# Input scaling and score-pad clearing leave GpSimd; the softmax division of the neighbourhood attention moves to ScalarE

## The chip, the cores and the metric

The kernel runs on one core of one Trainium2 chip. Its time is the device time of one execution in microseconds (us); the median of three runs counts. A core has five engines with a queue each, worked off in order: TensorE (PE in the profile; its weight loads are PEld), VectorE (DVE), ScalarE (ACT), GpSimd (POOL) and SyncE (SP), which here issues every data transfer (DMA).

## The reference

One encoder layer over 2048 tokens of width 1024, all in fp32:

```python
h = rmsnorm(x, g_mix)
z = h @ w_in                      # 1024 -> 5648, split into the branches' inputs and the gates
h_m   = mLSTM, forward and backward, from qk_m, v_m, o_m, i_pre, f_pre
h_na  = neighbourhood_attention(q_na, k_na, v_na, rpb)   # 8 heads of 32, window 8 x 16 on a 32 x 64 grid
h_mem = cross attention of q_mem into 256 memory tokens
y = g0 * (h_m @ w_proj_mlstm) + g1 * (h_na @ w_proj_na) + g2 * (h_mem @ w_proj_mem)
x = x + y @ w_out
out = x + square(relu(rmsnorm(x, g_ffn) @ w_up)) @ w_down
```

The change touches two places of it: `rmsnorm(x, g_mix)`, that is x times a factor per channel (`g_mix`) times a factor per token, and the softmax of the neighbourhood attention, `exp(s - max) / sum`.

## The kernel before

Every fp32 product is made of three matmuls (`mm3`, lines 241 to 243): each operand is split into a high part, which ScalarE writes, and a remainder, which VectorE writes. Weights arrive in units of 512 KB (`fetch`): DMA, ScalarE copy (L185), VectorE subtraction (L186). The work has three phases. Phase 1 (`phase_1`, 0 to some 850 us) takes the tokens in four blocks of 512 (`block_a`): it normalises a block, computes the inputs of all branches, and, woven in between, runs the attention into memory (`mem_unit`) and the neighbourhood attention (`na_stream`). Phase 2 is the mLSTM and the gates that are left, phase 3 the merge, the output projection and the MLP.

The order of TensorE's instructions is written out by hand: the program's order is the chip's. After every few matmuls a `tick` lets the woven streams put in one more step. The other engines' queues are ordered at compile time by a planner, which goes by each instruction's place in the program (its priority, which can be shifted, as by `LATER` around the weight splits) and by when it expects the operands to be there. Each queue then runs strictly in that order. In phase 1 the large products (24 matmuls each, `tok_group` and `ch_group`) go to two PSUM banks in turn (`mm=2`), which ScalarE mostly empties.

*Inputs.* Block 0 loads token-major tiles (`load_norm`). For blocks 1 to 3, `prep_x` loads a tile of 128 tokens that lies channel-major, `xT` (128 channels of one of 8 groups on the partitions; per partition 8 groups x 128 tokens), into one of two buffers `xt`, and GpSimd multiplies it twice (L428): by `gmix`, one factor per partition and group, and by `rb`, one factor per token, held in the tile `gbc`. There are 12 such tiles. For blocks 1 and 2 (`GATES_3`) the result is also stored (`s_raw`). `split_part` (L447 on ScalarE, L448 on VectorE) then splits it into `hT`, the operand of the block's matmuls. The factor per token comes from `rms_x`, which loads the same tokens again in the other layout and squares them on ScalarE (L457).

*Scores.* `na_scores` handles one head for 128 queries against 440 keys (320 in the first and last group of rows, g = 0 and g = 7): a matmul into PSUM (L1112), VectorE adds the bias and takes the extreme value in one instruction (L1115) into the score buffer `nsb`, ScalarE takes the exponential and its sum (L1117), VectorE the reciprocal (L1119) and the product with it (L1120, the softmax division), and GpSimd clears the pad behind the scores, up to the next multiple of 120 columns (L1123). There are 128 such heads. `nsb` is a rotating tile of three buffers. Four to five attention steps later `na_transpose` has TensorE transpose the buffer in pieces of 120 columns, pad included (L1131), and ScalarE or VectorE copies it out (L1134, L1136); `na_values` multiplies by the values (L1148). The bias tiles `nab` are loaded by DMA (L1103) into four buffers.

GpSimd's other work in phase 1 is `rstd` (L335, L336) and two products (L970, L1233), which stay.

Of the kernel before, what the change touches and what calls it, by code (L numbers as in the profile page):

```python
# [13 lines left out]
F32 = mybir.dt.float32  # L14
F32R = mybir.dt.float32r
BF16 = mybir.dt.bfloat16
AF = mybir.ActivationFunctionType
ALU = mybir.AluOpType
# [66 lines left out]
class Body:  # L85
# [296 lines left out]
    def phase_1(self):  # L382
        nc, a = self.nc, self.a
        p_a = self.p_a

        nc.scalar.activation(p_a.tile([128, 16], F32, name="warm"), self.mhalf, AF.Exp)
        self.xorder = [(0, t) for t in ORDER_0] + [(b, t) for b in range(1, NB) for t in range(4)]
        self.xhs = []
        self.hT = self.p_h.tile([128, 2, 8, TB], F32R, name="hT", tag="hT", bufs=1)
        self.mem_lanes = [(0,), (2,)]  # L390
        self.streams = [self.unit_stream(self.qkq, [(1, 3)]), self.unit_stream(self.memq, self.mem_lanes), self.na_stream()]
        self.mem_setup()
        self.bif = p_a.tile([16, 1], F32, name="bif")
        nc.sync.dma_start(self.bif, a["b_if"])
        cw = p_a.tile([128, 4, 6], F32, name="cw")
        nc.sync.dma_start(cw, a["conv_wb"])
        self.cw = p_a.tile([128, 4, 6], F32, name="cws")

        nc.vector.tensor_scalar(self.cw[:, 0:2], cw[:, 0:2], 1.0 / 16, None, ALU.mult)
        nc.vector.tensor_scalar(self.cw[:, 2:4], cw[:, 2:4], 0.5, None, ALU.mult)  # L400
        self.gmix = p_a.tile([128, 8], F32, name="gmix")
        nc.sync.dma_start(self.gmix, a["gT_mix"])
        self.halo = p_a.tile([128, 4, 4], F32, name="halo")
        nc.vector.memset(self.halo, 0.0)
        gna = p_a.tile([128, 2], F32, name="gna_raw")
        nc.sync.dma_start(gna, a["g_na"])
        self.gna = p_a.tile([128, 2], F32, name="gna")
        nc.vector.tensor_scalar(self.gna[:, 0:1], gna[:, 0:1], 32 ** -0.5, None, ALU.mult)
        nc.vector.tensor_copy(self.gna[:, 1:2], gna[:, 1:2])
        for b in range(NB):  # L410
            self.na_rate = NA_RATE[b]
            self.block_a(b)
        self.aux_end = self.na_end = True
        self.drain()

    def prep_x(self, gsrc=None, xt=None):

        if self.xorder:
            nc = self.nc
            b, t = self.xorder.pop(0)  # L420
            r0 = b * TB + t * 128
            if b == 0:
                self.xhs.append((self.load_norm(self.a["x"][r0:r0 + 128], self.gbc, gsrc, xt), t, False))
                return
            xt = self.x_tile(self.a["xT"][4 * b + t]).rearrange("p (k t) -> p k t", k=8)
            rb = self.rb[:, t * 128:(t + 1) * 128]
            for y in (self.gmix.unsqueeze(2), rb.unsqueeze(1)):
                nc.gpsimd.tensor_tensor(xt, xt, y.to_broadcast([128, 8, 128]), ALU.mult)  # L428
            if b in GATES_3:
                self.store(self.scr["raw"][b][:, :, t * 128:(t + 1) * 128], xt)  # L430
            self.xhs.append((xt, t, True))
# [674 lines left out]
    def na_scores(self, u, h):  # L1106
        nc = self.nc
        q, k = u["qk"]
        nk, c0 = u["nk"], 24 * u["half"]
        psc = self.ps("mx")  # L1110
        kl = k[:, h, :nk // 40 * 64].rearrange("p (r c) -> p r c", c=64)[:, :, c0:c0 + 40]
        nc.tensor.matmul(psc[:, :nk], q[:, h, u["half"] * 128:u["half"] * 128 + 128], kl, start=True, stop=True)  # L1112
        sb = self.t("nsb", [128, 480], 3)
        mx = self.small(1, "n")
        nc.vector.tensor_tensor_reduce(sb[:, :nk], psc[:, :nk], u["bias"][h][:, :nk], -1.0, 3e38, ALU.add, ALU.min, mx)  # L1115
        sm = self.small(1, "n")
        nc.scalar.activation(sb[:, :nk], sb[:, :nk], AF.Exp, scale=-1.0, bias=mx, accum_out=sm)  # L1117
        rs = self.small(1, "n")
        nc.vector.reciprocal(rs, sm)  # L1119
        nc.vector.tensor_scalar(sb[:, :nk], sb[:, :nk], rs, None, ALU.mult)  # L1120
        kp = len(u["kts"]) * 120
        if kp > nk:
            nc.gpsimd.memset(sb[:, nk:kp], 0.0)  # L1123
        return u, h, sb

    def na_transpose(self, u, h, sb):
# [650 lines left out]
```

## Time and profile before

| | |
|---|---|
| median of 3 runs | 2962.95 us (2962.1 to 2963.0) |
| the profiled execution | 2953.93 us; its span, first to last instruction, 2952.2 us |
| PE busy | 2861.8 us (97%) |
| DVE busy | 2092.6 us (71%) |
| ACT busy | 1218.8 us (41%) |
| POOL busy | 268.4 us (9%) |
| mean granted TensorE clock | 0.990 |

Busy times are shares of the profiled span, summed over phases with different limits. "Idle before, releaser" in a row is the time in which the row's engine did nothing before the instruction, and what ended it. The granted clock (PEclk) is the share of full speed at which TensorE was let run in a stretch. In the timeline several instructions of one line can be merged into one row (x2). DVE instructions that follow each other overlap a little at their ends, so a row can begin before the row above has ended.

### The profile page before, as it was taken

To read this page: it belongs to the slowest core of one execution; us is meant where nothing else is said; L and a number is where in the kernel's file an instruction comes from. 1 tells how busy PE (TensorE), PEld (TensorE's weight loads), DVE (VectorE), ACT (ScalarE), POOL (GpSimd) and SP (SyncE) were. 2 spreads that over 40 slices of the span, in tenths; PEclk is the share of its full clock that TensorE was granted. 3 is DMA by queue.
4 is the path that set the end of the run, shared out by engine and by line. 5 is a ranking of instruction groups with operands and counts; after the bars stand their busy time and mean duration, and the time that the engine had idled before them with its cause. 6 is when DMAs were issued, how large, how long until landed. Compare 5 with 4: busy or idle time off the path is not lost.

```text
span 2952.2 us, 41677 instructions
## 1 busy us (share of the span) xinstructions
PE 2861.8 (97%) x14908; PEld 2353.6 (80%) x14908; DVE 2092.6 (71%) x3490; ACT 1218.8 (41%) x2326; POOL 268.4 (9%) x406
## 2 busy tenths in 40 slices
PE   8999999999899989999999999999999999999999
PEld 7777787777677777888888888888888888888887
DVE  5867768676655667756688888666685988886666
ACT  6555556455433445343243333533312433344331
POOL 4231230320012321000000000000000000000000
PEclk9999999999999999999999999999999999999999
DMA  7866877677887895847435445756863444466554
GB/s 261 273 212 201 251 231 242 216 229 226 268 264 253 275 322 193 313 172 256 140 117 172 153 154 184 258 197 216 293 215 118 148 157 153 149 232 217 194 187 163
DMA packets 341487, 625.42 MB, mean 212 GB/s; under 512 B 29120, under 2 KB 150912, under 8 KB 340768
## 3 DMA queue, kind: packets, MB, share of 16 engines
q1 hardware_dynamic: 341280, 622.76, 64.5%
q8 instruction: 118, 1.93, 0.3%
q14 instruction: 89, 0.73, 0.1%
HBM read 446.03 MB, written 176.62 MB: 211 GB/s over the span
## 4 chain that ended last, share of the span: by engine, by line
PE 82%; DVE 6%; DMA 6%; issue 2%; ACT 2%; SPq 1%; POOL 1%; DVEq 0%; ACTq 0%; POOLq 0%
PE mm L241 25%; PE mm L242 25%; PE mm L243 25%; PE tr L1131 1%; DVE ws L186 1%; DMA nab<-in_rpb_dram 1%; PE pn L901 1%; DMA wr<-in_w_units_dram 1%; ACT ws L185 1%; PE mx L1148 1%; PE mx L1112 1%; PE pn L904 1%; DVE nsb L1115 1%; PE mm L1540 0%; DMA og<-s_o 0%
## 5 line engine op out<-in xcount | busy, mean ns | idle before, releaser
L242 PE MATMUL mm<-X,ws 128*128 128x512 f32 x1032 | 401.6, 389 | 1.4 <-DVE X L1368 1.4
L241 PE MATMUL mm<-X,ws 128*128 128x512 f32 x1032 | 401.9, 389 | 0.0
L243 PE MATMUL mm<-X,ws 128*128 128x512 f32 x1032 | 401.5, 389 | 0.0
L211 ACT ACTIVATE ws<-wr 128x512 fp32r<-128x512 f32 x294 | 176.7, 628 | 275.5 <-PE mm L243 179.7
L186 DVE TENSOR_TENSOR ws<-wr,ws 128x1024 fp32r<-128x1024 f32 (+1 forms) x160 | 203.5, 1280 | 85.8 <-ACT ws L185 85.5
L241 PE MATMUL mm<-ws,hT 128*128 128x512 f32 (+2 forms) x640 | 235.2, 367 | 5.8 <-ACT ws L185 3.0
L243 PE MATMUL mm<-X 128*128 128x512 f32 x616 | 239.7, 389 | 0.2 <-DVE X L1663 0.2
L242 PE MATMUL mm<-X 128*128 128x512 f32 x616 | 239.6, 389 | 0.0
L241 PE MATMUL mm<-X 128*128 128x512 f32 x616 | 239.6, 389 | 0.0
L242 PE MATMUL mm<-ws,hT 128*128 128x512 f32 (+2 forms) x640 | 228.3, 357 | 4.2 <-DVE ws L186 4.2
L243 PE MATMUL mm<-ws,hT 128*128 128x512 f32 (+2 forms) x640 | 227.7, 356 | 1.9 <-DVE hT L448 1.9
L242 PEld LDWEIGHTS mm<-X,ws 128*128 128x128 f32 x1032 | 193.7, 188 | 41.9 <-DVE X L1368 1.8
L243 PEld LDWEIGHTS mm<-X,ws 128*128 128x128 f32 x1032 | 193.7, 188 | 40.3
L241 PEld LDWEIGHTS mm<-X,ws 128*128 128x128 f32 x1032 | 193.7, 188 | 40.1
L185 ACT ACTIVATE ws<-wr 128x1024 fp32r<-128x1024 f32 (+1 forms) x160 | 168.2, 1057 | 110.1 <-PE mm L243 78.0
L212 DVE TENSOR_TENSOR ws<-wr,ws 128x512 fp32r<-128x512 f32 x294 | 197.9, 687 | 5.6 <-ACT ws L211 4.4
L1662 ACT ACTIVATE X<-X 128x1024 fp32r<-128x1024 f32 x109 | 115.7, 1062 | 197.1 <-DMA X<-s_t 72.8
L1663 DVE TENSOR_TENSOR X<-X 128x1024 fp32r<-128x1024 f32 x109 | 132.8, 1223 | 78.5 <-ACT X L1662 77.9
L1689 DVE TENSOR_TENSOR acc<-acc,mm 128x512 f32<-128x512 f32 x192 | 126.3, 683 | 66.3 <-PE mm L243 66.3
L241 PE MATMUL mm<-hT,ws 128*128 128x512 f32 x384 | 157.9, 411 | 0.7 <-ACT ev L624 0.7
L243 PE MATMUL mm<-hT,ws 128*128 128x512 f32 x384 | 151.0, 393 | 0.0
L242 PE MATMUL mm<-hT,ws 128*128 128x512 f32 x384 | 150.9, 393 | 0.0
(311 smaller groups left out, 6296.4 us busy)
## 6 DMA issues: line engine op xcount, KB each, us to landing
wr<-in_w_units_dram SPq DMA_DIRECT2D x276, 512.0 KB
s_s<-u SPq DMA_DIRECT2D x32, 1024.0 KB
s_g<-ev SPq DMA_DIRECT2D x96, 256.0 KB
ev<-s_g SPq DMA_DIRECT2D x96, 256.0 KB
s_a<-u SPq DMA_DIRECT2D x96, 256.0 KB
X<-s_s SPq DMA_DIRECT2D x45, 512.0 KB
nab<-in_rpb_dram SPq DMA_DIRECT2D x96, 220.0 KB
X<-s_a SPq DMA_DIRECT2D x32, 512.0 KB
```

The costliest lines, as they stand in the source:

```text
L185: nc.scalar.activation(w[:, 0], raw, AF.Copy)
L186: nc.vector.tensor_tensor(w[:, 1], raw, w[:, 0].bitcast(F32), ALU.subtract)
L211: nc.scalar.activation(hi, src, AF.Copy)
L212: nc.vector.tensor_tensor(lo, src, hi.bitcast(F32), ALU.subtract)
L241: mm(out, lhs[0], rhs[0], start=first, stop=False)
L242: mm(out, lhs[0], rhs[1], start=False, stop=False)
L243: mm(out, lhs[1], rhs[0], start=False, stop=last)
L901: mm(pn[h % 2][:, h // 2], pt[:, h], v1[:, h], start=h < 2, stop=first)
L904: mm(pn[h % 2][:, h // 2], qw[hp, h // 2], C[hp, h // 2], start=False, stop=True)
L1662: nc.scalar.activation(hi, src, AF.Copy)
L1663: nc.vector.tensor_tensor(lo, src, hi.bitcast(F32), ALU.subtract)
L1689: nc.vector.tensor_tensor(c, c, p, ALU.add)
```

## The change

`prep_x` no longer uses GpSimd: ScalarE multiplies by `gmix`, one instruction for each of the 8 channel groups (128 x 128 each, the factor read from a tile), and VectorE multiplies by `rb` in one instruction. The three score buffers become standing tiles that VectorE clears once at the start and that the heads use in turn. The softmax division becomes a ScalarE copy with the reciprocal as its scale. GpSimd's clearing of the pad is gone. The pad of a standing buffer stays zero as long as no longer row of scores was written over it; only for g = 7, whose 320 keys follow rows of 440, VectorE clears it (16 heads). Nothing else is edited; no DMA is added or taken away, and TensorE's order stays.

```diff
@@ phase_1
         self.gmix = p_a.tile([128, 8], F32, name="gmix")
         nc.sync.dma_start(self.gmix, a["gT_mix"])
+        self.nsb = [p_a.tile([128, 480], F32, name=f"nsb{i}") for i in range(3)]
+        for x in self.nsb:
+            nc.vector.memset(x, 0.0)
@@ prep_x
-            for y in (self.gmix.unsqueeze(2), rb.unsqueeze(1)):
-                nc.gpsimd.tensor_tensor(xt, xt, y.to_broadcast([128, 8, 128]), ALU.mult)
+            for k in range(8):
+                nc.scalar.activation(xt[:, k], xt[:, k], AF.Copy, scale=self.gmix[:, k:k + 1])
+            nc.vector.tensor_tensor(xt, xt, rb.unsqueeze(1).to_broadcast([128, 8, 128]), ALU.mult)
@@ na_scores
-        sb = self.t("nsb", [128, 480], 3)
+        self.nsb.append(self.nsb.pop(0))
+        sb = self.nsb[0]
         ...
-        nc.vector.tensor_scalar(sb[:, :nk], sb[:, :nk], rs, None, ALU.mult)
+        nc.scalar.activation(sb[:, :nk], sb[:, :nk], AF.Copy, scale=rs)
         kp = len(u["kts"]) * 120
-        if kp > nk:
-            nc.gpsimd.memset(sb[:, nk:kp], 0.0)
+        if u["g"] == 7:
+            nc.vector.memset(sb[:, nk:kp], 0.0)
```

## The prediction

> **What bounds the kernel now.** I read the page first, then the busy times by stretches of 100 us, then TensorE's waits, then the timeline around them.
>
> ```profile
> span 2952.2 us, 41677 instructions
> PE 2861.8 (97%) x14908; PEld 2353.6 (80%) x14908; DVE 2092.6 (71%) x3490; ACT 1218.8 (41%) x2326; POOL 268.4 (9%) x406
> ```
> ```profile
> 700.00:800.00 100.00, 87.22 (x648) 69.59 (x649) 64.78 (x179) 50.13 (x119) 3.74 (x28) 0.95 0.81 250
> sum 850.00, PE 792.18 PEld 648.33 DVE 585.80 ACT 448.87 POOL 194.54; mean PE 792.18 PEld 648.33 DVE 585.80 ACT 448.87 POOL 194.54
> ```
>
> TensorE bounds it: 97% busy, 90 us idle. All that the change touches lies in phase 1, the first 850 us (last row: one stretch from 0 to 850): there TensorE is idle for 850 - 792 = 58 us, and the granted clock falls short as well. No more than these 58 us and the lost clock can be gained; everything else stays TensorE's. So the question is which of TensorE's waits in phase 1 end otherwise.
>
> ```profile
> PE tr L1131 <- DVE nsb L1120: 15.2, 7, 6.4
> PE mx L1112 <- DVE sm L1115: 5.4, 3, 3.1
> PE mm L241 <- ACT ws L185: 3.0, 2, 2.3
> PE mx L1112 <- ACT me L1265: 2.6, 5, 1.0
> PE mm L241 <- ACT zif L538: 1.9, 2, 1.6
> ```
>
> No wait of TensorE names GpSimd. Yet GpSimd is behind the longest of those that name VectorE. Four places of the timeline, each with VectorE's, GpSimd's and TensorE's rows, and the clock in the stretch behind three of them:
>
> ```profile
> 169.85 3.00 DVE L448 TENSOR_TENSOR hT<-xt,hT 128x512 fp32r<-128x512 f32 x2
> 172.84 2.75 DVE L582 SCALAR_TENSOR_TENSOR ev<-ev,gbc 128x512 f32<-128x512 f32 x1
> 172.38 2.67 POOL L428 TENSOR_TENSOR xt<-xt,gbc 128x1024 f32<-128x1024 f32 x1
> 176.28 1.08 PE L1148 MATMUL mx<-npt,nav 120*32 120x128 f32 x16 [3.59 <-DVE mho L1291]
> 175.00:183.00 8.00, 6.72 (x38) 5.21 (x39) 5.06 (x15) 3.73 (x9) 3.23 (x4) 0.57 0.87 269
> ```
> ```profile
> 363.85 2.85 DVE L582 SCALAR_TENSOR_TENSOR ev<-ev,gbc 128x512 f32<-128x512 f32 x1
> 369.66 2.46 DVE L1120 TENSOR_SCALAR nsb<-nsb,sm 128x440 f32<-128x440 f32 x1
> 368.55 3.26 POOL L428 TENSOR_TENSOR xt<-xt,gbc 128x1024 f32<-128x1024 f32 x1
> 379.79 0.63 PE L1131 MATMUL tr<-ident,nsb 128*120 128x128 f32 x4 [1.93 <-DVE nsb L1120]
> 380.00:385.00 5.00, 5.00 (x21) 3.79 (x23) 4.12 (x13) 3.13 (x9) 0.13 (x1) 0.66 1.02 404
> ```
> ```profile
> 338.89 1.68 DVE L448 TENSOR_TENSOR hT<-xt,hT 128x512 fp32r<-128x512 f32 x1 [6.54 <-PE tr L1131]
> 341.75 1.09 PE L1287 MATMUL mx<-mpT,mv 128*64 128x128 f32 x16 [1.30 <-DVE sm L1115]
> 532.59 1.68 DVE L448 TENSOR_TENSOR hT<-xt,hT 128x512 fp32r<-128x512 f32 x1 [6.02 <-PE tr L1131]
> 537.15 0.53 PE L242 MATMUL mm<-ws,hT 128*128 128x512 f32 x1 [1.55 <-DVE ws L186]
> 536.00:542.00 6.00, 4.85 (x16) 3.98 (x17) 4.30 (x10) 4.34 (x9) 0.13 (x1) 0.72 0.70 205
> ```
> ```profile
> 560.36 6.24 DVE L186 TENSOR_TENSOR ws<-wr,ws 128x1024 fp32r<-128x1024 f32 x2
> 562.26 3.25 POOL L428 TENSOR_TENSOR xt<-xt,gbc 128x1024 f32<-128x1024 f32 x1
> 568.06 0.48 PE L1112 MATMUL mx<-nak,naq 96*128 96x440 f32 x1 [1.42 <-DVE nho L1155]
> 573.14 0.62 PE L1131 MATMUL tr<-ident,nsb 128*120 128x128 f32 x4 [1.81 <-DVE nsb L1120]
> ```
>
> The reader is to see that a VectorE instruction that meets GpSimd's scaling (L428) ends only after it: L582 began at 172.84, GpSimd's product ran from 172.38 to 175.05, L582 ended at 175.59. The same for L1120 at 369.66 (GpSimd until 371.81, L1120 until 372.12). VectorE then comes late to what TensorE needs, and behind the idle time the clock is cut to about half for some us.
>
> **The change part by part.** The rows for the costs:
>
> ```profile
> L428 POOL TENSOR_TENSOR xt<-xt,gmix 128x1024 f32<-128x1024 f32 x12 | 23.4, 1953 | 34.1 <-DMA xt<-in_xT_dram 17.8 <-DMA s_qk<-cy 13.6 <-issue 2.2
> L1123 POOL MEMSET nsb<- 128x40 f32 x128 | 18.1, 143 | 449.7 <-PE tr L1131 404.5 <-DVE sm L1115 16.5 <-DVE me L1268 15.9
> L1120 DVE TENSOR_SCALAR nsb<-nsb,sm 128x440 f32<-128x440 f32 x96 | 50.6, 527 | 1.3
> L448 DVE TENSOR_TENSOR hT<-tr,hT 128x512 fp32r<-128x512 f32 x8 | 5.5, 686 | 6.3 <-ACT hT L447 6.3
> L352 DVE TENSOR_TENSOR xt<-xt,gbc 128x1024 f32<-128x1024 f32 x2 | 2.4, 1220 | 0.4 <-DMA gbc<-in_g_mix_dram 0.4
> L1117 ACT ACTIVATE nsb<-nsb,sm 128x440 f32<-128x440 f32 x96 | 63.4, 661 | 93.7 <-DVE sm L1115 92.3 <-DVE halo L703 1.2
> L851 ACT ACTIVATE de<-rb,r_a 128x128 f32<-128x128 f32 x4 | 1.3, 397 | 0.0
> L457 ACT ACTIVATE xt<-xt 128x1024 f32<-128x1024 f32 x12 | 12.6, 1055 | 0.0
> L185 ACT ACTIVATE ws<-wr 128x1024 fp32r<-128x1024 f32 x93 | 96.9, 1052 | 19.8 <-DMA wr<-in_w_units_dram 13.3 <-PE mm L243 5.9
> ```
>
> 1. *GpSimd's 24 products go.* What that frees at the four places: an undisturbed 128x512 remainder takes 0.69 us (L448 from `tr`). At 170 to 176 two L448 take 3.00 and one L582 2.75 instead of some 3 x 0.69, 3.7 us lost, so all of the 3.59 goes. At 339 and 533 the loss is 1.68 - 0.69 = 1.0, so 1.0 of 1.30 and 1.0 of 1.55. At 362 to 372 the two rows shown lose (2.85 - 0.69) + (2.46 - 0.53) = 4.1, more than the 1.93 behind them. At 560 two weight remainders take 6.24 for about 2 x 1.22, 3.8 lost, above 1.42 + 1.81. Sum 3.59 + 1.0 + 1.93 + 1.0 + 3.23 = 10.8. The clock: 8 x 0.43 + 5 x 0.34 + 6 x 0.28 = 6.8. Together -17.6; I take -18. It is no more than that, since the other tiles left no idle time of TensorE that I can trace to them; at the least half, -9, if the new chain is itself late where the old one was.
>
> 2. *The new scaling.* Per tile eight ScalarE instructions with a factor per partition, the nearest row L851: 8 x 0.40 = 3.2 us, 38 us in all; and one VectorE product, 1.22 (L352). Chain per tile 4.4 us against 1.95 + 2.67 = 4.6 on GpSimd (L428 by `gmix`, and by `rb` at 172), so the store of `s_raw`, the SP queue behind it and L447 get the tile no later; no DMA is added or moved past another. VectorE's product waits behind ScalarE's eight and holds VectorE's queue meanwhile; both were in the same relation for each weight (L186 after L185).
>
> 3. *The division.* 128 ScalarE instructions of at most 0.66 (L1117, same shape, also a factor from a tile): 84 us onto ScalarE, 63 us off VectorE. Seven times TensorE waited for the division itself (15.2 us). There the chain grows by 0.66 less the 0.45 of an undisturbed L1120 (row below), 7 x 0.2 = +1.5; if each finds a weight split ahead of it in ScalarE's queue (1.05), +8.9. I take +3, two of seven.
>
> ```profile
> 361.00 0.45 DVE L1120 TENSOR_SCALAR nsb<-nsb,sm 128x440 f32<-128x440 f32 x1
> ```
>
> The Trainium skill speaks against this part: "ScalarE: Activation LUTs", "Rules for kernel authors", gives plain multiplications to VectorE. The rows agree on the length (0.66 against 0.45); by that rule alone only the +1.5 to +8.9 would be left of this part.
>
> 4. *VectorE relieved elsewhere.* 63 us fewer from the division. It can take back at most the 5.4 us that TensorE waits for L1115, at the least nothing, because a bias load can be what L1115 waits for. I take -3.
>
> 5. *ScalarE later elsewhere.* Its load in phase 1 goes from 449 to 449 + 84 + 38 = 571 us, 53% to 67%; the free share shrinks from 47% to 33%, and waits grow by about 47/33. TensorE's three waits for ScalarE shown sum to 7.5, so +3, and one or two cuts of the clock at 1.7 each: between 0 and +14 (doubled, with four cuts); I take +5.
>
> 6. *Pads and standing buffers.* 16 clearings and three at the start on VectorE cost at most 16 x 0.14 + 3 x 0.5 = 4 us, hidden while VectorE is free for 264 of 850 us. L1115 already had to wait for the transposes that read its buffer, so the standing buffers add no wait; what GpSimd's clearing waited for L1131 (404.5 us) held only GpSimd's own queue. Zero, no gain either, as no wait of TensorE names GpSimd.
>
> On what stays with GpSimd, "SBUF — State Buffer" of the Trainium skill ("Who interferes with whom") has VectorE instructions with two SBUF inputs blocked by any GpSimd instruction that reads SBUF: the new product is of that kind. L970 and L1233 still run, so a few such meetings remain; the sum stays the same by it.
>
> Sum: -18 + 3 - 3 + 5 = -13 on 2953.93 us, that is 2941 for a profiled execution (span 2952.2 plus 1.7 around it). The median of the runs is 9.0 above it, so 2950.
>
> **Rivals.** *ScalarE takes VectorE's place, no change.* 67% is what VectorE has now (586 of 850 = 69%). If ScalarE then makes TensorE wait as VectorE does now outside the four places (15.2 - 3.7 + 5.4 = 17 us instead of 7.5, and three cuts of the clock, 5 us), that is +15 against the -18: 2960, within the error. For it speaks that ScalarE empties TensorE's banks; against it that the weight splits, its largest group, are fetched ahead and can slide.
>
> *Slower: ScalarE stands before an input tile that has not landed.* L428 waited for the load itself, 17.8 us in 3 of 12 cases; GpSimd had nothing else to do, ScalarE does. A stop of 17.8/3 = 5.9 us plus the 3.2 us of scaling is 9.1. TensorE fills one of the two banks while the other is emptied, 24 matmuls at a step of 0.24 (rows below), some 5.6 us. Over 5.6 it waits: 3.5 plus a cut of the clock 1.7 = 5.2 per tile. It decides from stops of 2.4 us on; on 6 of 12 tiles it is +31, with the -18 and the rest at zero +13: 2976. Against it: L457 reads loads of the same kind on ScalarE, 12 times, with idle time 0.0 before it.
>
> ```profile
> 171.83 0.40 PE L241 MATMUL mm<-ws,hT 128*128 128x512 f32 x1
> 172.07 0.39 PE L242 MATMUL mm<-ws,hT 128*128 128x512 f32 x1
> ```
>
> *More.* VectorE's relief clears the crowded end as well: 700 to 800 has 12.8 us idle and 5 us of clock. With about two thirds of that, 12, and the 5.4 of L1115, -18 - 17 + 5 = -30: 2933.
>
> **How the numbers follow.** Forecast 0.55 (2940 to 2957), more 0.10, no change 0.16, slower 0.19. A difference under 0.2% (5.9 us) can't be told from none here. Faster 0.55 + 0.10 = 0.65, same 0.16, slower 0.19. The range goes from 2934, just above the rival with more, to 2972, which leaves out the worse half of the slower case and of the larger gain: about 0.15. The planner orders four queues of phase 1 anew, which the bounds must take in too.
>
> **What would show it.** Right: L582 and L448 at 0.7 us throughout, no TensorE wait of 3 us near 176, less cut clock before 600; ScalarE near 570 and VectorE near 526 us in the first 850 (586 - 63, - 12 lost at the places shown by others than L1120, + 15 for the product). Term 3 is wrong if waits of L1131 for the division exceed 18 us. The forecast is wrong if ScalarE shows idle time before the new scaling that ends with the landing of `xt`, or if TensorE's waits for ScalarE pass 20 us.

## The result, and the profile after

The changed kernel takes 2943.04 us in the median of 4 runs (2942.37 to 2944.39), beside 2962.52 us of the kernel before in the same comparison: a ratio of 0.9938, 95% interval 0.9921 to 0.9955, about 18 us. Run again on another chip, beside the kernel before on that chip, the ratio was 0.9955 (0.9938 to 0.9973), about 13 us; the two intervals overlap. The kernel before had medians of 2962.5, 2953.0, 2953.7 and 2958.3 us in the four comparisons of this study, which lie on different chips or occasions, so only ratios taken side by side are compared below; 0.1% is 3 us. Against itself the kernel before gave 1.0005 (0.9995 to 1.0015).

The changed kernel's page, first the span and the busy times, and then the stretch from 0 to 850 us (columns as in the stretches before: PE, PEld, DVE, ACT, POOL, granted clock, DMA share, GB/s):

```profile
span 2942.6 us, 41417 instructions
PE 2851.9 (97%) x14908; PEld 2346.9 (80%) x14908; DVE 2030.9 (69%) x3393; ACT 1314.9 (45%) x2550; POOL 198.0 (7%) x254
```
```profile
0.00:850.00 850.00, 795.43 (x5264) 652.10 (x5265) 532.54 (x1169) 550.10 (x1218) 125.53 (x136) 0.98 0.78 244
```

TensorE's work is the same 14908 matmuls in the same order, 9.9 us shorter in the profile, at a mean granted clock of 0.993 instead of 0.990. Its idle time is the same in this pair of profiles (2952.2 - 2861.8 = 90.4 us before, 2942.6 - 2851.9 = 90.7 after), so the whole difference of this pair lies in the time that the matmuls took, which a cut clock lengthens. The second profiles of the two kernels, each on another chip, have 98.0 and 87.4 us of idle time; one pair does not tell how the gain divides. In phase 1 VectorE gave up 53 us and ScalarE took 101. The lines of the new kernel lie a few numbers further down: L452 is the old L448, L586 the old L582, L1136 the old L1131, L1116 the old L1112. The instructions that stood beside GpSimd's products, and the new ones, in the groups of the first 850 us:

```profile
L452 DVE TENSOR_TENSOR hT<-xt,hT 128x512 fp32r<-128x512 f32 x24 | 16.2, 687 | 18.3 <-ACT hT L451 11.1 <-PE tr L1136 7.1
L586 DVE SCALAR_TENSOR_TENSOR ev<-ev,gbc 128x512 f32<-128x512 f32 x16 | 11.0, 687 | 7.3 <-ACT ev L585 6.5 <-DMA s_o<-ev 0.8
L431 ACT ACTIVATE xt<-xt,gmix 128x128 f32<-128x128 f32 x96 | 30.5, 398 | 1.2 <-DMA xt<-in_xT_dram 1.1
L1125 ACT ACTIVATE nsb<-nsb,sm 128x440 f32<-128x440 f32 x96 | 63.4, 660 | 14.2 <-DVE sm L1124 14.0
```

The first two rows say that in these groups nothing is stretched any more: the means of the 24 and of the 16 are the 0.69 us of the undisturbed form. What TensorE waits for in the whole execution, first the places with the division and with ScalarE, then its wait in phase 2:

```profile
PE tr L1136 <- ACT nsb L1125: 15.3, 8, 6.9
PE mm L241 <- ACT ws L185: 8.3, 3, 3.9
PE mx L1116 <- DVE sm L1120: 3.0, 2, 1.9
PE mx L1116 <- ACT me L1270: 2.0, 5, 0.8
PE mm L241 <- ACT zif L542: 2.0, 2, 1.6
PE tr L953 <- DVE h L949: 16.9, 8, 5.1
```

At the four places that the prediction had shown, the timeline and the clock now read (the first row is from the kernel before and follows the L1287 at 341.75):

```profile
343.55 0.51 PE L241 MATMUL mm<-ws,hT 128*128 128x512 f32 x1 [0.70 <-ACT ws L185]
```
```profile
171.37 0.39 PE L1116 MATMUL mx<-nak,naq 96*128 96x320 f32 x1 [1.46 <-DVE mho L1296]
330.01 1.09 PE L1292 MATMUL mx<-mpT,mv 128*64 128x128 f32 x16 [0.35 <-DVE sm L1120]
331.54 2.43 ACT L431 ACTIVATE xt<-xt,gmix 128x128 f32<-128x128 f32 x8
333.87 1.04 ACT L185 ACTIVATE ws<-wr 128x1024 fp32r<-128x1024 f32 x1
334.97 0.79 PE L241 MATMUL mm<-ws,hT 128*128 128x512 f32 x1 [3.87 <-ACT ws L185]
368.24 0.65 PE L1136 MATMUL tr<-ident,nsb 128*120 128x128 f32 x4 [1.87 <-ACT nsb L1125]
373.37 0.60 PE L1136 MATMUL tr<-ident,nsb 128*120 128x128 f32 x4
527.69 0.50 PE L241 MATMUL mm<-ws,hT 128*128 128x512 f32 x1 [2.84 <-ACT ws L185]
529.14 0.73 PE L242 MATMUL mm<-ws,hT 128*128 128x512 f32 x1 [0.95 <-DVE ws L186]
559.00 0.65 PE L1136 MATMUL tr<-ident,nsb 128*120 128x128 f32 x4 [0.90 <-ACT nsb L1125]
```
```profile
175.00:183.00 8.00, 8.00 (x41) 6.60 (x40) 3.66 (x12) 5.74 (x14) 5.93 (x4) 1.00 0.97 300
334.00:342.00 8.00, 6.37 (x17) 4.86 (x18) 5.07 (x9) 6.31 (x12) 0.00 (x0) 0.57 0.72 214
```

A row near the same time need not be the same matmul, so the waits are compared by their place in TensorE's order, which is the same in both kernels. The six waits that the prediction had named, 11.6 us in sum, are nearly gone: the matmuls that had waited 3.59, 1.93 and 1.81 us start without a wait (the second of them is the transpose at 373.37), and 1.30, 1.55 and 1.42 became 0.35, 0.95 and 0.14. That is 10.2 us less. But other matmuls close by now wait: 1.46 us at 171, 1.87 at 368 (the transposes ahead of those at 373.37), 0.90 at 559, and for a weight's split 3.87 near 331, where it had been 0.70, and 2.84 near 525, where the same matmul had not waited. That is 10.2 us more; three smaller waits in these stretches fell by 1.7. The clock stayed whole near 175 and was cut near 334 instead, by 0.43 of 8 us, 3.4 us. TensorE waits near 331 and 525 for a weight whose split stands in ScalarE's queue behind the eight scalings of an input tile (331.54 to 333.97, then L185).

### The profile page after: what moved, and what is told of

The parts are those of the page before. It is cut to its first block, busy times and chain, and to the rows that moved or that the text cites. A ratio compares the mean times of both kernels' runs of the same rounds, so it can differ in the third digit from the quotient of the medians.

```text
span 2942.6 us, 41417 instructions
## 1 busy us (share of the span) xinstructions
PE 2851.9 (97%) x14908; PEld 2346.9 (80%) x14908; DVE 2030.9 (69%) x3393; ACT 1314.9 (45%) x2550; POOL 198.0 (7%) x254
## 3 DMA queue, kind: packets, MB, share of 16 engines
q8 instruction: 118, 1.93, 0.3%
## 4 chain that ended last, share of the span: by engine, by line
PE 83%; DMA 5%; DVE 5%; ACT 4%; issue 2%; SPq 1%; POOL 0%; DVEq 0%; ACTq 0%; POOLq 0%
PE mm L241 26%; PE mm L242 25%; PE mm L243 25%; PE tr L1136 2%; DMA rb<-s_r 1%; ACT ws L185 1%; DVE ws L186 1%; PE mx L1153 1%; PE mx L1116 1%; PE pn L905 1%; DMA wr<-in_w_units_dram 1%; ACT nsb L1122 1%; PE mm L1545 0%; DMA v<-s_v 0%; DMA hf<-s_hf 0%
## 5 line engine op out<-in xcount | busy, mean ns | idle before, releaser
L186 DVE TENSOR_TENSOR ws<-wr,ws 128x1024 fp32r<-128x1024 f32 (+1 forms) x160 | 196.1, 1233 | 99.1 <-ACT ws L185 95.9
L185 ACT ACTIVATE ws<-wr 128x1024 fp32r<-128x1024 f32 (+1 forms) x160 | 168.4, 1059 | 98.9 <-PE mm L243 77.7
```

The source lines that it names most:

```text
L185: nc.scalar.activation(w[:, 0], raw, AF.Copy)
L186: nc.vector.tensor_tensor(w[:, 1], raw, w[:, 0].bitcast(F32), ALU.subtract)
```

## The experiments

The theory under test was that GpSimd's products held up VectorE (A). Its rivals were that the relief of VectorE by the moved division is the gain (B), and that the clearing of pads in GpSimd's queue was the cost (C).

**The parts alone.** Four kernels on one chip.

The new input scaling alone:

```diff
 # the kernel before
-            for y in (self.gmix.unsqueeze(2), rb.unsqueeze(1)):
-                nc.gpsimd.tensor_tensor(xt, xt, y.to_broadcast([128, 8, 128]), ALU.mult)
+            for k in range(8):
+                nc.scalar.activation(xt[:, k], xt[:, k], AF.Copy, scale=self.gmix[:, k:k + 1])
+            nc.vector.tensor_tensor(xt, xt, rb.unsqueeze(1).to_broadcast([128, 8, 128]), ALU.mult)
```

> The kernel before with the new input scaling alone (ScalarE by gmix, VectorE by the factor per token); division on VectorE, pads cleared by GpSimd as before. Theory A (GpSimd's scaling held up VectorE, and its going is the gain): 11 to 18 us under the kernel before, no VectorE instruction stretched over 2 us in the first 850 us. Rival B (the relief of VectorE by the moved division is the gain): within 5 us of the kernel before. Rival C (the pads' clearing in GpSimd's queue was the cost): within 5 us as well.

Measured: 0.9987 (0.9978 to 0.9997), 4 us. In these two groups of VectorE (first 850 us) nothing is stretched any more, as A said:

```profile
L449 DVE TENSOR_TENSOR hT<-xt,hT 128x512 fp32r<-128x512 f32 x24 | 16.4, 685 | 18.4 <-PE tr L1132 12.9 <-ACT hT L448 5.5
L583 DVE SCALAR_TENSOR_TENSOR ev<-ev,gbc 128x512 f32<-128x512 f32 x16 | 11.0, 686 | 3.0 <-ACT ev L582 2.2 <-DMA xt<-in_xT_dram 0.8
```

but the gain is a third of the least that A had named. (The profiled execution, 2943.24 us, is one of the fastest of the ten, 2941.66 to 2954.15, so these rows need not show what the median run lost.) TensorE's waits for L185 have grown already, from 3.0 to 7.1 us, and that for the division is where it was:

```profile
PE mm L241 <- ACT ws L185: 7.1, 3, 3.0
PE tr L1132 <- DVE nsb L1121: 16.0, 7, 7.5
```

The division alone:

```diff
 # the kernel before
-        nc.vector.tensor_scalar(sb[:, :nk], sb[:, :nk], rs, None, ALU.mult)
+        nc.scalar.activation(sb[:, :nk], sb[:, :nk], AF.Copy, scale=rs)
```

> The kernel before with the softmax division alone moved to ScalarE; GpSimd scales and clears as before. Theory A: within 5 us of the kernel before, and L582, L448 and L186 still stretched to 2.4 to 3.4 us beside GpSimd's products. Rival B: 12 to 20 us faster. Rival C: within 5 us.

Measured: 1.0011 (0.9999 to 1.0024). No gain; the stretched instructions remain (L582 with a mean of 805 ns, in the row below; single ones of L582, L448 and L186 take up to 2.3, 2.9 and 3.3 us), and B falls.

```profile
L582 DVE SCALAR_TENSOR_TENSOR ev<-ev,gbc 128x512 f32<-128x512 f32 x16 | 12.9, 805 | 5.8 <-ACT ev L581 5.8
```

The standing buffers alone:

```diff
 # the changed kernel, scaling and division as before
-            for k in range(8):
-                nc.scalar.activation(xt[:, k], xt[:, k], AF.Copy, scale=self.gmix[:, k:k + 1])
-            nc.vector.tensor_tensor(xt, xt, rb.unsqueeze(1).to_broadcast([128, 8, 128]), ALU.mult)
+            for y in (self.gmix.unsqueeze(2), rb.unsqueeze(1)):
+                nc.gpsimd.tensor_tensor(xt, xt, y.to_broadcast([128, 8, 128]), ALU.mult)
-        nc.scalar.activation(sb[:, :nk], sb[:, :nk], AF.Copy, scale=rs)
+        nc.vector.tensor_scalar(sb[:, :nk], sb[:, :nk], rs, None, ALU.mult)
```

> The kernel before with the standing score buffers alone; division on VectorE, scaling on GpSimd. Theory A and rival B: within 4 us of the kernel before. Rival C (rstd and the scaling stood behind clearings that waited for transposes): 8 us or more faster.

Measured: 0.9995 (0.9983 to 1.0006): no difference, and C falls.

The changed kernel with the division back on VectorE:

```diff
 # the changed kernel
-        nc.scalar.activation(sb[:, :nk], sb[:, :nk], AF.Copy, scale=rs)
+        nc.vector.tensor_scalar(sb[:, :nk], sb[:, :nk], rs, None, ALU.mult)
```

> The changed kernel with the division back on VectorE. Theory A with a division that is worth nothing: 2943 within 4 us, like the changed kernel. If the division costs by its longer chain and ScalarE's load (terms 3 and 5 of the forecast): 2935 to 2939. Rival B: 2956 or more.

Measured: 0.9974 (0.9960 to 0.9987), 8 us, at a median of 2945.8 us, which is within the 4 us of the first reading. The three parts alone sum to -0.13 + 0.11 - 0.05 = -0.07% on this chip. All together brought -0.62% and -0.45%, but on other occasions: the whole change was not run on the chip of the parts, so how far the parts fall short of it is not shown exactly; it is taken up below.

**The whole change again, and what the scaling costs where it now stands.** Four kernels on a second chip.

> The changed kernel itself once more, beside the kernel before on the same chip. If the 19 us between the two medians are the change's: 17 to 21 us under the kernel before. If the sum of terms is right (lock-outs gone, two of them bought back by new waits for ScalarE): 8 to 14 us under it.

Measured: 0.9955 (0.9938 to 0.9973), 13 us, in the range that the sum of terms had given.

No ScalarE work added at all:

```diff
 # the changed kernel
-            for k in range(8):
-                nc.scalar.activation(xt[:, k], xt[:, k], AF.Copy, scale=self.gmix[:, k:k + 1])
-            nc.vector.tensor_tensor(xt, xt, rb.unsqueeze(1).to_broadcast([128, 8, 128]), ALU.mult)
+            for y in (self.gmix.unsqueeze(2), rb.unsqueeze(1)):
+                nc.vector.tensor_tensor(xt, xt, y.to_broadcast([128, 8, 128]), ALU.mult)
-        nc.scalar.activation(sb[:, :nk], sb[:, :nk], AF.Copy, scale=rs)
+        nc.vector.tensor_scalar(sb[:, :nk], sb[:, :nk], rs, None, ALU.mult)
```

> Standing buffers, division on VectorE, and both scalings of a tile on VectorE: no ScalarE instruction is added at all. If ScalarE's eight scalings standing ahead of a weight split cost time (TensorE's waits for L185 near 331 and 525 in the changed kernel, 3.9 and 2.8 us and the clock cut behind them): those two waits gone, 3 to 8 us faster than the changed kernel with the division back on VectorE, 10 to 16 us under the kernel before. If VectorE's load is what counts: 2 to 6 us slower than that kernel.

Measured: 0.9951 (0.9935 to 0.9966), 14 us under the kernel before, the same as the changed kernel. The time lies in the range of the first reading, but not for its reason: the two waits did not go. They moved to the matmul behind and to the other engine (timeline of VectorE and TensorE):

```profile
330.82 1.22 DVE L431 TENSOR_TENSOR xt<-xt,gmix 128x1024 f32<-128x1024 f32 x1
332.07 1.22 DVE L431 TENSOR_TENSOR xt<-xt,gbc 128x1024 f32<-128x1024 f32 x1
333.75 1.22 DVE L186 TENSOR_TENSOR ws<-wr,ws 128x1024 fp32r<-128x1024 f32 x1
335.02 0.80 PE L242 MATMUL mm<-ws,hT 128*128 128x512 f32 x1 [3.29 <-DVE ws L186]
529.28 0.50 PE L242 MATMUL mm<-ws,hT 128*128 128x512 f32 x1 [2.98 <-DVE ws L186]
```

So it is not ScalarE's load that makes TensorE wait there. Whichever engine scales the tile, the scaling stands ahead of that engine's half of the weight split (on VectorE with one L1119 of 0.61 us between). This run also speaks against B once more: VectorE is busy for 593 us of the first 850, more than the 586 of the kernel before, and the gain is there.

Both scalings on VectorE and the division on ScalarE:

```diff
 # the changed kernel
-            for k in range(8):
-                nc.scalar.activation(xt[:, k], xt[:, k], AF.Copy, scale=self.gmix[:, k:k + 1])
-            nc.vector.tensor_tensor(xt, xt, rb.unsqueeze(1).to_broadcast([128, 8, 128]), ALU.mult)
+            for y in (self.gmix.unsqueeze(2), rb.unsqueeze(1)):
+                nc.vector.tensor_tensor(xt, xt, y.to_broadcast([128, 8, 128]), ALU.mult)
```

> The changed kernel with both scalings on VectorE and the division on ScalarE. If the eight scalings are what costs on ScalarE and the division is worth nothing: like the kernel with no added ScalarE work, within 3 us. If the division costs 3 to 8 us by its chain and load: slower than that kernel by as much.

Measured: 0.9966 (0.9951 to 0.9981), 0.15% above the kernel with no added ScalarE work, with intervals that overlap. Alone the division cost 0.11%, on top of this scaling 0.15%, on top of ScalarE's scaling it gained 0.19% (0.9974 to 0.9955, on two chips). It has no price of its own that these runs could fix.

The scaling put later in the planner's order:

```diff
 # the changed kernel, prep_x
+            prio = self.tc.cur_priority
+            self.tc.cur_priority = prio + 2 * LATER
             for k in range(8):
                 nc.scalar.activation(xt[:, k], xt[:, k], AF.Copy, scale=self.gmix[:, k:k + 1])
             nc.vector.tensor_tensor(xt, xt, rb.unsqueeze(1).to_broadcast([128, 8, 128]), ALU.mult)
+            self.tc.cur_priority -= 2 * LATER
```

> The changed kernel with the three lines of scaling put later in the planner's order (priority shifted by twice LATER), so that weight splits go ahead of them; no work changes. If it is only their place ahead of a weight split that costs: the waits for L185 near 331 and 525 are under 1 us, and it is 3 to 8 us faster than the changed kernel. If the scaled tile is then late for L451: TensorE waits for L451 or L452 there instead, and it is the same or slower.

Measured: 0.9957 (0.9942 to 0.9972), the same time; the expected gain of 3 to 8 us did not come, and the waits are not under 1 us. But they show what they are made of (ScalarE and TensorE):

```profile
338.04 1.55 ACT L433 ACTIVATE xt<-xt,gmix 128x128 f32<-128x128 f32 x5
339.50 1.04 ACT L185 ACTIVATE ws<-wr 128x1024 fp32r<-128x1024 f32 x1
340.44 0.97 ACT L433 ACTIVATE xt<-xt,gmix 128x128 f32<-128x128 f32 x3
340.59 0.50 PE L241 MATMUL mm<-ws,hT 128*128 128x512 f32 x1 [2.99 <-ACT ws L185]
533.07 0.55 PE L241 MATMUL mm<-ws,hT 128*128 128x512 f32 x1 [1.96 <-ACT ws L185]
```

Three of the eight scalings now stand behind the split, at a step of 0.29 us each (2.43 - 0.40 over 7), 0.87 us; the waits fell from 3.87 to 2.99 and from 2.84 to 1.96, by 0.88 both times.

**Is it GpSimd's products, or the tile's way through GpSimd?** Two kernels on a third chip. In the idle products below, GpSimd multiplies the tile after it has been scaled and writes a scratch tile; this is work added, and nobody reads the result.

```diff
 # the changed kernel; the control has only the edits above prep_x
+        self.junk = p_a.tile([128, 4, 128], F32, name="junk")
+        nc.vector.memset(self.junk[:, 0, 0:2], 0.0)
-            pT = self.t("mpT", [128, 4, 128], 4)
+            pT = self.t("mpT", [128, 4, 128], 3)
 # prep_x, behind the scaling
+            for g in range(2):
+                x = xt[:, 4 * g:4 * g + 4]
+                for y in (self.gmix[:, 4 * g:4 * g + 4].unsqueeze(2), rb.unsqueeze(1)):
+                    nc.gpsimd.tensor_tensor(self.junk, x, y.to_broadcast([128, 4, 128]), ALU.mult)
```

> The changed kernel with one buffer fewer for the memory attention's transposed scores (3 instead of 4), which makes room for the scratch tile of the next kernel. Both theories: within 4 us of the changed kernel.

> The control with GpSimd busy again for nothing: for each of the 12 input tiles it makes four products of 128 x 512 from the scaled tile into a scratch tile that nobody reads, about as long as its two products of before. Nothing in the chain of the computation waits for them but the next load into the same buffer. If GpSimd's products hold up VectorE's instructions and that was the cost: VectorE instructions beside them stretched by 0.5 to 1.5 us, 20 us or more in all, and 5 to 15 us slower than the control. If what was slow was the chain of the tile through GpSimd: within 3 us of the control.

Measured: the control 0.9960 (0.9946 to 0.9975), like the changed kernel; with the idle products 1.0015 (1.0002 to 1.0027). The idle products cost 0.55%, 16 us, as much as the whole change had gained. In the groups of the first 850 us (the last row is one of GpSimd's two kinds of product by itself, with the least, middle and longest duration in ns), VectorE's remainder of the tile in the control:

```profile
L454 DVE TENSOR_TENSOR hT<-xt,hT 128x512 fp32r<-128x512 f32 x24 | 16.1, 686 | 18.5 <-ACT hT L453 11.3 <-PE tr L1138 7.1
```

and with the idle products:

```profile
L458 DVE TENSOR_TENSOR hT<-xt,hT 128x512 fp32r<-128x512 f32 x24 | 26.9, 1133 | 17.5 <-ACT hT L457 10.4 <-PE tr L1142 7.1
L438 POOL TENSOR_TENSOR junk<-xt,gbc 128x512 f32<-128x512 f32 x24 | 38.7, 1613 | 1.9
L438 POOL TENSOR_TENSOR junk<-xt,gmix 128x512 f32<-128x512 f32 x24 | 36.2, 1507 | 311.1 <-DVE xt L434 259.4 <-DVE sm L1130 45.8 <-issue 4.7
```
```profile
L438 POOL TENSOR_TENSOR junk<-xt,gbc x24: 1274/1598/2338, 105.1 to 578.5; 128x512 f32<-128x512 f32 x24
```

The busy times of the two whole executions, of the control (span 2941.2 us) and then of the kernel with the idle products (span 2957.2):

```profile
PE 2854.5 (97%) x14908; PEld 2349.2 (80%) x14908; DVE 2030.5 (69%) x3394; ACT 1313.9 (45%) x2550; POOL 193.9 (7%) x254
```
```profile
PE 2858.6 (97%) x14908; PEld 2351.1 (80%) x14908; DVE 2056.6 (70%) x3394; ACT 1314.6 (44%) x2550; POOL 271.2 (9%) x302
```

The timeline at two of the places, of the control and then of the kernel with the idle products:

```profile
172.01 0.38 PE L1118 MATMUL mx<-nak,naq 96*128 96x320 f32 x1 [1.39 <-DVE mho L1298]
561.10 0.65 PE L1138 MATMUL tr<-ident,nsb 128*120 128x128 f32 x4 [1.14 <-ACT nsb L1127]
```
```profile
169.27 3.19 DVE L458 TENSOR_TENSOR hT<-xt,hT 128x512 fp32r<-128x512 f32 x2
168.35 1.90 POOL L438 TENSOR_TENSOR junk<-xt,gmix 128x512 f32<-128x512 f32 x1
176.06 0.60 PE L1122 MATMUL mx<-nak,naq 96*128 96x320 f32 x1 [5.80 <-DVE mho L1302]
573.50 1.11 PE L1142 MATMUL tr<-ident,nsb 128*120 128x128 f32 x4 [3.21 <-ACT nsb L1131]
```

The same 24 remainders take 1133 instead of 686 ns, and the same 3394 VectorE instructions of the execution 26 us longer in all. The wait near 172 goes from 1.39 to 5.80 us, that of the transposes at 561 and 573 from 1.14 to 3.21; TensorE's idle time grows by 11.9 us (86.7 to 98.6), its busy time by 4.1. VectorE and ScalarE did not have to wait for the idle products in this kernel, except for one wait of 1.4 us, VectorE's scaling of a later tile. And in the first 850 us the instructions of ScalarE, VectorE and SyncE, and GpSimd's others, stand in the same order in both traces, so it is not another order of the queues that costs. Theory A stands: GpSimd's products stretch VectorE's instructions, and TensorE pays. The 16 us are the price of these idle products; they occupy GpSimd for 36.2 + 38.7 = 74.9 us, a third more than the 23.4 + 32.1 = 55.5 us of its products in the kernel before.

**The weight splits ahead.** One more kernel on the third chip:

```diff
 # the changed kernel, phase_1
+        self.later = 0
         for b in range(NB):
             self.na_rate = NA_RATE[b]
             self.block_a(b)
+        self.later = LATER
```

> The changed kernel with the weight splits of phase 1 no longer put back in the planner's order (shift 0 instead of 60). If the waits for L185 near 331 and 525 come from the split's low rank behind attention and scaling: they go, 3 to 8 us faster than the changed kernel. If they come from the planner expecting the weight or its buffer later than it is: they stay, within 4 us, or it is slower because splits now stand ahead of evictions.

Measured: 0.9956 (0.9942 to 0.9970), like the changed kernel, and the two waits are unchanged (3.86 and 2.83 us). The split's rank in the planner's order is not what puts it behind the scaling. Of the two readings the second is left, that the planner expects the weight or its buffer later than it is; no run shows what it expects.

The kernel before against itself, on the same chip:

> The kernel before against itself, for what a comparison here can tell: a ratio of 1.000 with an interval of some 0.15% to each side. Its profile shows which of TensorE's waits in phase 1 come back at the same place: if all the places of the forecast do (near 176, 342, 380, 537, 568, 573), each single profile can be read to about 1 us there.

Measured: 1.0005 (0.9995 to 1.0015). In this second profile of the kernel before the waits near 342 (1.31 us), 380 (1.93), 537 (1.54), 568 (1.43) and 573 (1.85) are back to a few hundredths; that near 176 is smaller, 1.83 instead of 3.59 us.

## Why the prediction was right

The sign, the range and the cause were right. The sum of terms, -13, is what the second comparison measured (0.9955 of 2953.7 is 13 us); the first measured 18 (0.9938). Point by point:

1. *GpSimd's products, -18.* The mechanism was right: the stretch is gone, and the six waits named fell by 10.2 us where 10.8 were counted. The term as a whole is not confirmed in size. The clock at the places named, -6.8, came back only near 175, and new waits of 10.2 us close by took the idle time back; only those for L185 are in the terms below (5). By the runs the products are worth between 4 us (taken out alone) and 14 (with both scalings on VectorE); put back idle, and a third longer, they cost 16. The size of one place in one profile is no firm number either: in the second profile of the kernel before the wait near 176 is 1.83 instead of 3.59 us. Nor is every VectorE instruction that meets GpSimd's product held until its end. In these rows of the kernel before, L1115, which reads one tile from PSUM and one from SBUF, takes 0.60 us in the middle of a product, as its group does on average (0.61):

```profile
366.63 0.60 DVE L1115 CUSTOM_DVE_ANT_0 nsb<-mx,nab 128x440 f32<-128x440 f32 x1
366.29 2.18 POOL L428 TENSOR_TENSOR xt<-xt,gmix 128x1024 f32<-128x1024 f32 x1
```

2. *The scaling.* 0.40 us for one ScalarE scaling was right (398 ns), 3.2 us for eight was not: they follow at 0.29 and take 2.43. VectorE's product took the 1.22 of its row. That the store gets the tile no later does not hold everywhere: in phase 1 SyncE's queue waited 19.5 us in four waits for VectorE's product, 14.5 of them before the store at 335, where GpSimd's products had held it for 4.9 in all. TensorE's waits that name a load did not grow by it (2.6 us in sum before, 2.4 after).
3. *The division, +3.* Mis-sized: TensorE waits 15.3 us for it as before (15.2), so 0 in the place where it was looked for. By the times its effect changes sign with what stands beside it, and no size stands clear of the noise.
4. *VectorE relieved, -3.* The wait for L1115 fell from 5.4 to 3.0: -2.4. With the division back on VectorE it is 4.3, so some half of this is the division's.
5. *ScalarE later, +5.* The three waits shown went from 7.5 to 12.3, +4.8 where +3 was counted; with the 3.4 us of clock lost behind one of them that is +8.2, within the bounds of 0 to +14. The reason was not the load (with no work added on ScalarE the matmuls behind wait 3.3 and 3.0 us for VectorE), but the scaling ahead of the weight split in one queue, so that the size came near was luck.
6. *Pads, zero.* 0.9995.

The predicted 2950 is 7 us above the measured 2943. In that comparison the kernel before had 2962.5, as the prediction took it, so the 7 us lie in the difference: -13 against a measured -18 to -19. On the second chip, where the kernel before had 2953.7, the difference was -13. The changed kernel had nearly the same median both times (2943.0 and 2942.4). Why the kernel before was 9 us slower on the first occasion no run shows; the 9.0 us that the prediction laid on top of its profiled execution are of this kind.

Of the rivals, the slower one did not happen: ScalarE's idle time before the new scaling that ended with the landing of the tile is 1.1 us in all. ScalarE did not take VectorE's place (550 us busy in 850, predicted 570), and the crowded end from 700 to 800 us did not clear: its longest wait is 6.9 us, before 6.4. One sign of being wrong was put too loosely: TensorE's waits for ScalarE past 20 us. The three waits shown sum to 12.3; with the division, which is now ScalarE's, to 27.6, and the kernel is faster all the same.

What stays open is the price of GpSimd's products in the kernel before. Taking them out alone brought 4 us, with the standing buffers 8, with both scalings on VectorE 14, and the whole change 13 to 18. Every part has its own order of the queues, and the chips differ; these runs do not separate the two. TensorE's wait for L949 in phase 2 (L945 in the kernel before), 12.5 and 15.9 us in two profiles of the kernel before, 16.9 and 17.9 in two of the changed one, may have given a little of the gain back; two profiles each do not settle it.

## What to carry to other kernels

Work given to an idle engine need not be free for the others: look in the timeline for instructions of VectorE whose durations differ from their own form's, and for the GpSimd instruction beside which they end. When work is moved to another queue, ask what it will stand in front of there; the wait that grew was a weight split behind the moved scaling, on either engine. And to test such a stall, put the suspected instructions back with nobody reading them: that separates the contention from the chain of data. It gives the price of what is put back, so compare its length with what was there. And compare waits by the instruction's place in the program's order: near the same time another one may stand.

## What was not expected

GpSimd is held as well: its 128 x 512 product took 1613 ns on average beside the busy VectorE, and 1274 at the least. "SBUF — State Buffer" of the Trainium skill, "Who interferes with whom", says that whichever of the two starts first blocks the other. The rows agree that each is held by the other (GpSimd's product 1613 against 1274 ns, VectorE's remainder 1133 against 686); which of two had started first they do not show.

Eight small ScalarE instructions in a row cost 2.43 us, not eight times 0.40. "ScalarE: Activation LUTs" of the Trainium skill, "What ACT_TABLE_LOAD costs", says that such instructions overlap by about 93 ns; here the step of 0.29 to the duration of 0.40 shows 0.11.
